# A hybrid encoder layer on one core: x also arrives transposed, one sum writes both attention patches, attention runs at another rate

## The chip, the cores and the metric

The kernel runs on one core of one Trainium2 chip. The metric is device microseconds from start to end of one execution. PE is the matrix engine, PEld its weight loads, DVE the vector engine, ACT the scalar engine, POOL GpSimd, and SP the engine that issues most DMAs.

## What is computed

One layer over T = 2048 tokens of D = 1024 channels, all in fp32:

```
h = rms_norm(x, norm_g)                    # mean of squares over the channels of a token
z = h @ w_in                               # 1024 x 10240
a, qkv, c, d, gates, merge = split(z)
y = [fourier(a), neighborhood_attention(q, k, v, rpb), conv_module(c), spatial_gating(d)]
merged = sum_n sigmoid(merge[n]) * ((y[n] * silu(gates[n])) @ w_branch[n])
out = rms_norm(x + merged @ w_out, final_g)
```

The attention works on a grid of 32 rows by 64 columns, 8 heads of 64 channels, with a window of 8 x 16 around each token.

## The kernel before

**Products.** Every large product is made of three matmuls on a high and a low part of each operand (`mm3`, line L238). `split` makes the parts: ACT casts the high one (L226), DVE subtracts it from the source for the low one (L227).

**The z phase** computes z in two halves of 1024 tokens, each in 20 blocks of 512 columns. A block takes seven products instead of eight, in the order B11, B21, T1, T2, B22, T3, T4; each has two parts of 12 matmuls of 512 columns (the first blocks, which come out turned, use 24 of 256). The names stand for quarters of normalised, transposed x and their differences T1 to T4: `hH` and `hL` are the two parts of such an operand, four tiles each. The operands are used by all blocks of a half. Weights arrive as `wq` tiles, get summed (L230) and split, five parts ahead.

**x in the kernel before.** `x_load` brings eight tiles `xn` of 128 tokens x 1024 channels. `x_square` (L468) squares a tile on ACT and sums along its row into `ss`; `x_rstd` makes 1 / root of it; `x_gain` spreads `norm_g` over the partitions with two matmuls against ones (L464); `x_scale` (L473) multiplies by both on DVE. An operand is then turned: for each of its four tiles, four transposes on PE (`x_turn_tile`, L504) fill one of three PSUM banks `p`, and `split` reads the bank. `first` places the steps in block 0 of the first half, before the products that need them (T2 is turned twice there). For the second half, block 17 of the first half loads and normalises x (`x_norm`, one step per turn of the side `xl`, whose rate is 2.0 per product step), GpSimd makes the differences, and `swap` and `swapped` turn the operands in the last block of the first half (19) and the first block of the second, as each old operand comes free.

**Order.** The code is written in program order; `tick` advances side work (a list of generators with rates) between matmuls, and a scheduler then fixes each engine's queue. Every engine works through its queue in order, SP's DMAs too.

**The y phase** projects eight blocks: for each half the branches 3, 2, 0, 1. A block is 8 x 4 steps of six matmuls (weights `yw`, gate tiles `sg`). Attention is side work here: each step advances it by `ATT_RATE[0]` pieces until block (0, 1), by `ATT_RATE[1]` after. A piece is the scores of one patch (L998), the turn of its probabilities (L1020), or the turn and `apply` (L1036). `apply` adds two partial results in `ot` and writes two patches of 8 x 16 tokens into the tile `ya` with two DVE sums (L1046, the patches stand reversed). The output of a head of the first half is stored to `yd` (`yd_77` is that of heads 6 and 7) and read back as `yL` by the next block; `fetch` advances attention until the heads that it wants are done. `gated` loads the gates of branch 1 into `bg`, which has one buffer.

## Time and profile before

| | |
|---|---|
| median of 3 runs | 2475.91 us (2474.22 to 2477.24) |
| the profiled execution, its own time | 2475.09 us |
| its span in the trace | 2473.3 us |
| mean granted clock of PE | 0.993 |
| PE busy | 2384.8 us, 96% of the span |
| DVE, ACT, POOL busy | 69%, 49%, 14% |

The span is what the trace covers; the rest of the execution's own time lies around it. The clock is a share of the full 2.4 GHz. A wait is named by the engine or DMA whose signal came last, and idle time of an engine other than the bottleneck costs nothing by itself. The mean of a matmul or a transpose is the time from its start to its modelled end; these overlap, so what one costs is read from the distance of starts.

### The profile page before, as it was taken

The numbers are of one execution on the slowest core, as the hardware profiler recorded it, in microseconds if no ns is written. First come the engines' busy times: TensorE is split into PE (matmuls) and PEld (weight loads), VectorE is DVE, ScalarE is ACT, GpSimd is POOL, SyncE is SP. The second block draws the span as 40 slices with busy tenths as digits, with TensorE's granted clock in tenths as the row PEclk, the third lists the DMA queues.
The fourth block names the chain that finished last, engine by engine and source line by source line (L and its number), as shares of the span: only waits on it lengthen the run. The fifth ranks groups of instructions, "written<-read, shape, count | busy, mean of one in ns | idle before, by whom it ended". The sixth has DMA issues, their size and how long they took to land. (4 is left out here: it accounts for less than half of the span.)

```text
span 2473.3 us, 34008 instructions
## 1 busy us (share of the span) xinstructions
PE 2384.8 (96%) x11804; PEld 1987.8 (80%) x11804; DVE 1699.2 (69%) x2945; ACT 1205.7 (49%) x2251; POOL 341.7 (14%) x290
## 2 busy tenths in 40 slices
PE   7999999999999999999999989999999999999998
PEld 6998778888877899878778867887777778778786
DVE  7585799997566637459979567673677775556542
ACT  5343545544584534354554465443666645654112
POOL 1000000000322100000000230001245433222220
PEclk9999999999999999999999999999999999999999
DMA  4353766655474335376774477777988978986776
GB/s 164 124 160 128 249 223 234 216 179 184 156 282 152 134 127 140 117 228 190 231 227 164 152 227 266 245 244 245 279 292 242 274 245 280 284 283 214 246 249 217
DMA packets 253015, 525.07 MB, mean 212 GB/s; under 512 B 26150, under 2 KB 120742, under 8 KB 252204
## 3 DMA queue, kind: packets, MB, share of 16 engines
q1 hardware_dynamic: 198572, 451.58, 56.2%
q10 hardware_dynamic: 54272, 71.32, 8.1%
q8 instruction: 93, 1.52, 0.3%
q14 instruction: 78, 0.64, 0.1%
HBM read 351.49 MB, written 171.31 MB: 211 GB/s over the span
## 5 line engine op out<-in xcount | busy, mean ns | idle before, releaser
L226 ACT CAST whi<-wq 128x512 fp32r<-128x512 f32 x560 | 347.0, 621 | 492.8 <-PE z L238 279.2
L227 DVE TENSOR_TENSOR wlo<-wq,whi 128x512 fp32r<-128x512 f32 x560 | 392.6, 703 | 268.3 <-ACT whi L226 258.8
L238 PE MATMUL z<-hH,whi 128*128 128x512 f32 x1088 | 427.7, 393 | 4.2 <-ACT b L374 4.0
L238 PE MATMUL z<-hH,wlo 128*128 128x512 f32 x1088 | 424.9, 391 | 3.2 <-DVE wlo L227 3.2
L238 PE MATMUL z<-hL,whi 128*128 128x512 f32 x1088 | 424.4, 390 | 0.0
L238 PE MATMUL b<-hH,whi 128*128 128x512 f32 x816 | 323.4, 396 | 16.1 <-DVE zu L233 15.9
L238 PE MATMUL b<-hH,wlo 128*128 128x512 f32 x816 | 319.7, 392 | 3.7 <-DVE wlo L227 3.7
L238 PE MATMUL b<-hL,whi 128*128 128x512 f32 x816 | 319.4, 391 | 0.0
L238 PE MATMUL z<-yH,yw 128*128 128x512 f32 x1024 | 305.8, 401 | 11.5 <-ACT yH L226 6.8
L786 DVE SCALAR_TENSOR_TENSOR acc<-hb,cw,acc 128x1009 f32<-128x1009 f32 (+1 forms) x240 | 306.9, 1282 | 2.0 <-ACT acc L782 1.5
L238 PEld LDWEIGHTS z<-hH,whi 128*128 128x128 f32 x1088 | 204.5, 188 | 47.5 <-ACT b L374 6.2
L238 PEld LDWEIGHTS z<-hH,wlo 128*128 128x128 f32 x1088 | 204.3, 188 | 46.8 <-DVE wlo L227 3.9
L238 PEld LDWEIGHTS z<-hL,whi 128*128 128x128 f32 x1088 | 204.5, 188 | 40.1
L238 PEld LDWEIGHTS z<-yH,yw 128*128 128x128 f32 x1024 | 191.8, 191 | 55.9 <-ACT yH L226 10.4
L238 PEld LDWEIGHTS b<-hH,whi 128*128 128x128 f32 x816 | 153.8, 188 | 54.7 <-DVE zu L233 16.1
L985 POOL TENSOR_TENSOR e<-mask,gt 128x512 f32<-128x512 bf16 x96 | 137.1, 1458 | 431.8 <-DMA gt<-in_rp_dram 360.3
L238 PEld LDWEIGHTS b<-hH,wlo 128*128 128x128 f32 x816 | 153.9, 189 | 36.8 <-DVE wlo L227 4.4
L238 PEld LDWEIGHTS b<-hL,whi 128*128 128x128 f32 x816 | 154.0, 189 | 30.4
L238 PE MATMUL z<-yL,yw 128*128 128x512 f32 x512 | 166.3, 401 | 2.7 <-DVE yL L227 2.4
L1007 ACT ACTIVATE sc<-sc,mn 128x512 f32<-128x512 f32 x128 | 92.5, 723 | 140.3 <-DVE mn L1004 140.2
L1004 DVE CUSTOM_DVE_ANT_0 sc<-p,e 128x512 f32<-128x512 f32 x128 | 87.1, 684 | 58.0 <-PE p L998 38.7
L238 PE MATMUL z<-yw,mH 128*128 128x512 f32 x384 | 119.7, 393 | 2.4 <-DMA yw<-wo 2.4
(228 smaller groups left out, 4123.2 us busy)
## 6 DMA issues: line engine op xcount, KB each, us to landing
wq<-in_wz_dram SPq DMA_DIRECT2D x140, 512.0 KB, 3.9
wk<-wq SPq DMA_DIRECT2D x80, 512.0 KB, 2.7
wq<-wk SPq DMA_DIRECT2D x80, 512.0 KB, 3.9
yw<-wb SPq DMA_DIRECT2D x64, 512.0 KB, 5.5
sg<-md SPq DMA_DIRECT2D x64, 512.0 KB, 5.0
yw<-wo SPq DMA_DIRECT2D x64, 512.0 KB, 4.2
vt<-vd SPq DMA_DIRECT2D x64, 320.0 KB, 7.4
md<-zs ACTq DMA_DIRECT2D x64, 256.0 KB, 3.5
```

Of the source, the lines that this page charges most:

```text
L226: nc.scalar.copy(hi, src)
L227: (eng or nc.vector).tensor_tensor(out=lo, in0=src, in1=hi.bitcast(F32), op=ALU.subtract)
L238: mm = lambda *a, **kw: self.nc.tensor.matmul(*a, skip_group_check=chained, **kw)
L786: nc.vector.scalar_tensor_tensor(out=a, in0=hb[:, j:j + n], scalar=self.cw[:, i, j:j + 1], in1=a, op0=ALU.mult, op1=ALU.add)
L985: nc.gpsimd.tensor_tensor(out=ev, in0=mv, in1=gv, op=ALU.subtract)
L1004: nc.vector.tensor_tensor_reduce(out=s2, in0=ps, in1=e, scale=1.0, scalar=3.0e38, op0=ALU.add, op1=ALU.min, accum_out=mn)
L1007: nc.scalar.activation(out=s2, in_=s2, func=AF.Exp, scale=-1.0, bias=mn[:, 0:1], accum_out=sm)
```

## The change

x comes a second time, transposed, as input `xt` (8 tiles of 128 channels x 2048 tokens), and `norm_g` as a constant of 128 x 8. The kernel's own input still gives the rows, but for the squares alone.

- `x_rows` loads `xt` into the eight `xn` tiles, in two parts of 512 tokens each.
- `x_square` loads a row tile of 128 x 512 into the ring `zs` (four buffers, shared with the results of the products) and squares it there; 16 of them fill `ss`.
- `x_rstd(c, banks)` adds the two sums of a token, takes root and reciprocal, multiplies the identity by the four columns (`d`, one more `zs` tile), and lets PE multiply ones by `d`, so that each partition has the factor of every token; ACT copies it to `t1`. At the start the product is made twice.
- `x_scale` multiplies an `xt` tile by the channel's gain (a scalar per partition) and by that factor.
- `x_split` splits from SBUF; the transposes and their PSUM banks are gone. The differences of operands are taken from the same places by the same engines.
- In the attention, `ph` and `pl` hold the two patches in reversed order, so that one sum of 64 x 16 x 16 writes both.
- `ATT_RATE[0]` goes from 1.6 to 1.75.

The diff, cut to its core:

```diff
...
 FFT_RATE = (1.15, 2.3)
-ATT_RATE = (1.6, 0.74)
+ATT_RATE = (1.75, 0.74)
 X_AT = 17
...
         x=np.asarray(x)[0],
+        xt=np.asarray(x)[0].T.reshape(KT, P, T),
         wz=wz, wb=wb, wo=wo, rp=rp,
-        ng=np.asarray(norm_g).reshape(1, D),
+        ng=np.asarray(norm_g).reshape(KT, P).T,
         cw=np.asarray(conv_w)[0].reshape(TAPS, 4, P).transpose(2, 1, 0),
...
+    def x_load(self, half):
+        self.t1 = self.xp.tile([P, 4, 512], F32, name="t1", tag="t1")
+        self.ss = self.zp.tile([P, 16], F32, name="ss", tag="ss", bufs=2)
+        self.xs = [self.xp.tile([P, 2, 512], F32, name="xn", tag="xn", bufs=8) for _ in range(KT)]
+        self.xt_at = half * HALF
+    def x_rows(self, k, c):
+        t0 = self.xt_at + 512 * c
+        self.load(self.xs[k][:, c], self.io["xt"][k, :, t0:t0 + 512])
+    def x_square(self, j, i):
+        t0 = self.xt_at + j * P
+        r = self.zs()
+        self.load(r, self.io["x"][t0:t0 + P, 512 * i:512 * i + 512])
+        self.nc.scalar.activation(out=self.t1[:, 0], in_=r, func=AF.Square, accum_out=self.ss[:, 8 * i + j:8 * i + j + 1])
+    def x_rstd(self, c, banks):
+        nc = self.nc
+        s, more = self.ss[:, 4 * c:4 * c + 4], self.ss[:, 8 + 4 * c:12 + 4 * c]
+        self.tt(s, s, more, ALU.add)
+        self.rstd(s, s, 1.0 / D)
+        d = self.zs()
+        for j in range(4):
+            at = slice(j * P, (j + 1) * P)
+            nc.vector.tensor_scalar(out=d[:, at], in0=self.ident, scalar1=s[:, j:j + 1], scalar2=None, op0=ALU.mult)
+        for bank in banks:
             ps = bank()
-            self.nc.tensor.matmul(ps, self.ones[0:1, :], row, start=True, stop=True)
-            self.nc.scalar.copy(self.t1[:, 2 + i], ps)
-    def x_square(self, j):
-        self.nc.scalar.activation(out=self.t1[:, 0:2].rearrange("p a c -> p (a c)"), in_=self.xs[j], func=AF.Square,
-                                  accum_out=self.ss[:, j:j + 1])
-    def x_scale(self, j, i):
-        xv = self.xs[j][:, 512 * i:512 * i + 512]
-        self.nc.vector.scalar_tensor_tensor(out=xv, in0=xv, scalar=self.ss[:, j:j + 1], in1=self.t1[:, 2 + i],
+            nc.tensor.matmul(ps, self.ones, d, start=True, stop=True)
+        nc.scalar.copy(self.t1[:, 2 + c], ps)
+    def x_scale(self, k, c):
+        xv = self.xs[k][:, c]
+        self.nc.vector.scalar_tensor_tensor(out=xv, in0=xv, scalar=self.ng[:, k:k + 1], in1=self.t1[:, 2 + c],
                                             op0=ALU.mult, op1=ALU.mult)
...
     def x_norm(self):
-        for j in range(8):
-            self.x_square(j)
-            yield
-        self.x_rstd(range(8))
-        for j in range(8):
-            for i in range(2):
-                self.x_scale(j, i)
+        for c in range(2):
+            for j in range(4 * c, 4 * c + 4):
+                for i in range(2):
+                    self.x_square(j, i)
+                    yield
+            for k in range(KT):
+                self.x_rows(k, c)
+                if k % 2:
+                    yield
+        for c in range(2):
+            self.x_rstd(c, (self.psp,))
+            yield
+        for c in range(2):
+            for k in range(KT):
+                self.x_scale(k, c)
                 yield
-    def x_parts(self, j, which):
-        a, b = self.xs[j], self.xs[4 + j]
-        return dict(B11=a[:, :512], B21=a[:, 512:], B12=b[:, :512], B22=b[:, 512:], T2=a[:, :512], T3=b[:, :512],
-                    T4=a[:, 512:], T1=self.t1[:, j])[which]
+    def x_parts(self, k, which):
+        a, b = self.xs[k], self.xs[4 + k]
+        return dict(B11=a[:, 0], B21=b[:, 0], B12=a[:, 1], B22=b[:, 1], T2=a[:, 0], T3=a[:, 1],
+                    T4=b[:, 0], T1=self.t1[:, k])[which]
     def x_sums(self, which, eng):
...
         a, b = dict(T1=("B12", "B11"), T3=("B22", "B12"), T2=("B22", "T1"), T4=("B21", "T2"))[which]
...
+    def x_split(self, which):
         self.X[which] = []
         for k in range(4):
-            if done:
-                ps = done[k]
-            else:
-                ps = self.psp()
-                for j in range(4):
-                    self.x_turn_tile(ps, which, j, k)
             hh = self.hp.tile([P, 512], F32R, name="hH", tag="hH" + which, bufs=4)
             hl = self.hp.tile([P, 512], F32R, name="hL", tag="hL" + which, bufs=4)
-            self.split(hh, hl, ps)
+            self.split(hh, hl, self.x_parts(k, which))
             self.X[which].append((hh, hl))
...
         self.ident = self.const("t_ident", [P, P])
-        self.x_load(0, range(1))
+        self.ng = self.const("ng", [P, KT])
+        self.x_load(0)
         self.rstd(self.ss[:, 0:1], self.eps, 1.0)
-        self.x_gain(self.psb)
-        self.x_load(0, range(1, 4))
         self.wq = {}
         self.w_gen, self.w_ahead = self.weights(), []
-        for i in range(4):
-            self.w_load(0, i)
-        self.x_load(0, range(4, 8))
         xl, mix, conv, fft, pre = (self.side(r) for r in (2.0, MIX_RATE, CONV_RATE[0], FFT_RATE[0], PRE_RATE))
...
         self.conv_side, self.fft_side = self.sides[2:4]
-        ps = [(self.psz if k < 2 else self.psp)() for k in range(4)]
         for j in range(4):
-            self.x_square(j)
-            self.x_rstd([j])
-            self.x_scale(j, 0)
-            for k in range(4):
-                self.x_turn_tile(ps[k], "B11", j, k)
+            for i in range(2):
+                self.x_square(j, i)
+        self.w_load(0, 0)
+        for k in range(4):
+            self.x_rows(k, 0)
+        for i in range(1, 4):
+            self.w_load(0, i)
+        for k in range(4, KT):
+            self.x_rows(k, 0)
+        self.x_rstd(0, (self.psb, self.psb))
         self.w_more()
-        xl.append(self.x_turn("B11", ps))
-        self.drain(xl)
-        for j in range(4):
-            self.x_scale(j, 1)
+        self.X["B11"] = []
+        split = self.x_split("B11")
+        for k in range(4):
+            self.x_scale(k, 0)
+            next(split)
+        for _ in split:
+            pass
         for _ in range(W_BUFS - 2):
             self.w_more()
+        for j in range(4, 8):
+            for i in range(2):
+                self.x_square(j, i)
+        for k in range(KT):
+            self.x_rows(k, 1)
         self.cw = self.const("cw", [P, 4, TAPS], self.zp)
...
             if i == 0:
-                xl.append(self.x_turn("B21"))
-                self.drain(xl)
-                for j in range(4, 8):
-                    self.x_square(j)
-                    self.x_rstd([j])
-                    self.x_scale(j, 0)
-                    self.x_scale(j, 1)
+                split = self.x_split("B21")
+                for k in range(4):
+                    self.x_scale(4 + k, 0)
+                    next(split)
+                for _ in split:
+                    pass
+                self.x_rstd(1, (self.psp,))
+                for k in range(KT):
+                    self.x_scale(k, 1)
                 xl.append(self.x_sums("T1", nc.vector))
                 self.drain(xl)
-                xl.append(self.x_turn("T1"))
+                xl.append(self.x_split("T1"))
             elif i == 1:
                 xl.append(self.x_sums("T2", nc.vector))
-                xl.append(self.x_turn("T2"))
+                xl.append(self.x_split("T2"))
             elif i < len(ORDER) - 1:
-                xl.append(self.x_turn(ORDER[i + 1]))
+                xl.append(self.x_split(ORDER[i + 1]))
                 if i == 2:
...
             if i:
-                xl.append(self.x_turn(ORDER[i - 1]))
+                xl.append(self.x_split(ORDER[i - 1]))
                 if i < 3:
...
                 self.drain(xl)
-                xl.append(self.x_turn(ORDER[-1]))
+                xl.append(self.x_split(ORDER[-1]))
         last = len(BLOCKS) - 1
...
                     open_pool("xp")
-                    self.x_load(1, range(8))
-                    self.x_gain(self.psp)
+                    self.x_load(1)
                     xl.append(self.x_norm())
...
             pt = pt.rearrange("p (b q) -> p b q", b=4)
-            nc.scalar.copy(ph[:, ri], pt)
-            nc.vector.tensor_tensor(out=pl[:, ri], in0=pt, in1=ph[:, ri].bitcast(F32), op=ALU.subtract)
+            nc.scalar.copy(ph[:, 1 - ri], pt)
+            nc.vector.tensor_tensor(out=pl[:, 1 - ri], in0=pt, in1=ph[:, 1 - ri].bitcast(F32), op=ALU.subtract)
             if ri == 1:
...
             for b in (1, 2, 3):
-                nc.tensor.matmul(po, vt[:, b], both[:, :, b:b + 4:3], start=b == 1, stop=False)
-            for ri, b, bi in ((0, 0, 0), (1, 4, 3)):
-                nc.tensor.matmul(po[:, :, ri], vt[:, b], pp[:, :, ri, bi], start=False, stop=ri == 1)
+                nc.tensor.matmul(po, vt[:, b], both[:, :, b - 1:b + 5:5], start=b == 1, stop=False)
+            for a, b, bi in ((1, 0, 0), (0, 4, 3)):
+                nc.tensor.matmul(po[:, :, a], vt[:, b], pp[:, :, a, bi], start=False, stop=a == 0)
             if cw == 0:
...
             nc.vector.tensor_tensor(out=t_, in0=po[0:64, 1], in1=t_, op=ALU.add)
-            for ri in range(2):
-                nc.vector.tensor_tensor(
-                    out=yt[:, 8 * ri:8 * ri + 8, 16 * cw:16 * cw + 16],
-                    in0=po[0:64, 0, ri, ::-1].rearrange("p (r c) -> p r c", r=8),
-                    in1=t_[:, ri, ::-1].rearrange("p (r c) -> p r c", r=8), op=ALU.add)
+            back = lambda t: t.rearrange("p a q -> p (a q)")[:, ::-1].rearrange("p (r c) -> p r c", r=16)
+            nc.vector.tensor_tensor(out=yt[:, :, 16 * cw:16 * cw + 16], in0=back(po[0:64, 0]), in1=back(t_), op=ALU.add)
             if cw == 3:
...
```

What moves in the queues shows at three places. **SP at the start**; `xn` are tiles of x (`xt` after), `zs` the ring, `wq` weights. Before:

```order
L210 DMA t_ident<-in_t_ident_dram 128x128
L210 DMA xn<-in_x_dram 128x1024
L210 DMA zs<-in_ng_dram 1x512 x2
L210 DMA xn<-in_x_dram 128x1024 x3
L210 DMA wq_262<-in_wz_dram 128x1024
```

After, from the row tiles of the second 512 tokens on (the first eight stand ahead, with four weight tiles and eight of `xt`):

```order
L211 DMA zs<-in_x_dram 128x512 [waits DMAHW6_49,Activation_49]
L211 DMA zs<-in_x_dram 128x512 [waits DMAHW7_49,Activation_49]
L211 DMA zs<-in_x_dram 128x512 [waits DMAHW0_49,Activation_49]
L211 DMA zs<-in_x_dram 128x512 [waits DMAHW1_49,DVE_49,PE_49]
L211 DMA xn<-in_xt_dram 128x512 [waits DMAHW2_49]
L217 DMA wk<-wq_286 128x1024 [waits DMAHW3_49,DVE_49]
L211 DMA zs<-in_x_dram 128x512 [waits DMAHW6_49,DMAHW4_49,Activation_49]
L211 DMA zs<-in_x_dram 128x512 [waits DMAHW7_49,DMAHW5_49,Activation_49]
```

The row tiles now wait for ACT's squares of the tiles before them in the ring; the fourth waits for DVE and PE, who fill and read the diagonal `d` in the same buffer, and the last four stand behind the store of a weight sum.

**ACT in block 17**, where the squares of the second half (L468, after L461) stand among the copies and casts of the products. Before:

```order
L468 ACTIVATE t_6990,ss<-xn 128x1024 [waits DMAHW4_49,DMAHW2_49,Pool_49]
L374 COPY b<-z 128x512 [waits PE_49]
L468 ACTIVATE t_6990,ss<-xn 128x1024 [waits DMAHW2_49,Activation_49]
L226 CAST whi<-wq_6676 128x512
L468 ACTIVATE t_6990,ss<-xn 128x1024 [waits DMAHW4_49,Activation_49]
```

After:

```order
L461 ACTIVATE t_6878,ss<-zs 128x512 [waits DMAHW3_49,DMAHW2_49,DMAHW5_49,DMAHW0_49,Pool_49]
L375 COPY b<-z 128x512 [waits PE_49]
L461 ACTIVATE t_6878,ss<-zs 128x512 [waits DMAHW3_49,Activation_49]
L461 ACTIVATE t_6878,ss<-zs 128x512 [waits DMAHW4_49,Activation_49]
L227 CAST whi<-wq_6738 128x512 [waits DVE_49,PE_49]
L461 ACTIVATE t_6878,ss<-zs 128x512 [waits DMAHW5_49,Activation_49]
```

There are 16 squares instead of 8, each behind its own load, with two between two casts where one stood. Later in the block, DVE's last scales (L480) have moved ahead of the two additions (L234) that free the banks of T3 and T4:

```order
L480 SCALAR_TENSOR_TENSOR xn<-xn,ng,t_6878 128x512 [waits DMAHW7_49]
L234 TENSOR_TENSOR zu<-z,zu 128x512 [waits PE_49]
L228 TENSOR_TENSOR wlo<-wq_7140,whi 128x512 [waits DMAHW4_49,Activation_49]
L480 SCALAR_TENSOR_TENSOR xn<-xn,ng,t_6878 128x512 [waits DMAHW0_49]
L480 SCALAR_TENSOR_TENSOR xn<-xn,ng,t_6878 128x512 [waits DMAHW1_49]
L234 TENSOR_TENSOR zu<-b,zu 128x512 [waits PE_49]
```

**SP at the entry into the last projection of the first half**; `yd_77` is the output of the last two heads, `vt`, `ks`, `qs` are operands of the next heads. Before:

```order
L216 DMA yd_77<-ya 64x1024
L210 DMA sg<-md_171 128x1024
L210 DMA yw<-wb_118 128x1024
L210 DMA yL<-yd_76 128x1024
L210 DMA yL<-yd_77 128x1024
L210 DMA vt<-vd 128x640
L210 DMA bg<-gd_92 128x1024
L210 DMA ks<-kd_65 64x1024
```

After:

```order
L211 DMA yw<-wb_118 128x1024
L211 DMA yL<-yd_76 128x1024
L217 DMA yd_74<-ya 64x1024
L211 DMA yL<-yd_77 128x1024
L211 DMA bg<-gd_92 128x1024
L211 DMA vt<-vd 128x640
L211 DMA sg<-md_173 128x1024
L211 DMA ks<-kd_65 64x1024
```

The store of the last heads stood four rows ahead of its load; it now stands 21 rows ahead, and in its place there is a store of the first head of the second half.

## Rows read from the trace of the kernel before

**Rows 1.** The page, its first and its sixth part (KB each, us to landing).

```profile
PE 2384.8 (96%) x11804; PEld 1987.8 (80%) x11804; DVE 1699.2 (69%) x2945; ACT 1205.7 (49%) x2251; POOL 341.7 (14%) x290
...
wq<-in_wz_dram SPq DMA_DIRECT2D x140, 512.0 KB, 3.9
```

**Rows 2.** Groups by line on PE: busy us, mean ns | idle before, releasers.

```profile
L504 PE MATMUL p<-t_ident,xn 128*128 128x128 f32 x200 | 33.7, 294 | 3.9 <-DVE hL L227 2.4 <-DVE xn L230 1.3 <-DVE xn L473 0.2
...
L504 PE MATMUL p<-t_ident,t 128*128 128x128 f32 x32 | 5.7, 299 | 2.1 <-DVE t L230 1.6 <-DVE hL L227 0.4
...
L504 PE MATMUL z<-t_ident,xn 128*128 128x128 f32 x8 | 2.7, 442 | 2.0 <-DVE xn L473 2.0
```

**Rows 3.** Timeline of PE, last block of the first half: start us, us.

```profile
792.11 0.39 PE L238 MATMUL z<-hL,whi 128*128 128x512 f32 x1
...
792.79 0.39 PE L238 MATMUL z<-hL,whi 128*128 128x512 f32 x1
...
839.85 0.60 PE L504 MATMUL p<-t_ident,xn 128*128 128x128 f32 x4
...
840.99 0.60 PE L504 MATMUL p<-t_ident,xn 128*128 128x128 f32 x4
```

**Rows 4.** Views of one line: ns min/median/max, first and last start.

```profile
L473 DVE SCALAR_TENSOR_TENSOR xn<-xn,ss,t x32: 734/744/1781, 9.9 to 758.6; 128x512 f32<-128x512 f32 x32
...
L227 DVE TENSOR_TENSOR wlo<-wq,whi x560: 621/684/1769, 13.8 to 1696.1; 128x512 fp32r<-128x512 f32 x187
...
L1046 DVE TENSOR_TENSOR ya<-p,ot x128: 259/273/284, 1748.9 to 2281.4; 64x128 f32<-64x128 f32 x128
```

**Rows 5.** Stretch 40 to 60: us, PE, PEld, DVE, ACT, POOL busy, clock, DMA, GB/s.

```profile
40.00:60.00 20.00, 16.37 (x116) 15.06 (x116) 18.54 (x23) 8.20 (x15) 6.59 (x4) 0.89 0.14 54
```

**Rows 6.** Timeline of the start, all engines.

```profile
5.20 1.06 ACT L468 ACTIVATE t<-xn 128x1024 f32<-128x1024 f32 x1 [2.88 <-DMA xn<-in_x_dram]
...
5.43 3.75 PE L464 MATMUL b<-zs,ones 1*128 1x512 f32 x4 [5.43 <-DMA zs<-in_ng_dram]
...
16.31 0.58 PE L238 MATMUL z<-whi,hH 128*128 128x256 f32 x1
```

**Rows 7.** Timeline of the first block, all engines.

```profile
37.24 0.38 PE L238 MATMUL z<-whi,hH 128*128 128x256 f32 x1 [0.46 <-ACT hH L226]
...
41.55 4.67 DVE L230 TENSOR_TENSOR xn<-xn,t 128x512 f32<-128x512 f32 x4
...
42.48 6.59 POOL L230 TENSOR_TENSOR xn<-xn 128x512 f32<-128x512 f32 x4 [42.04 <-DVE xn L230]
...
84.26 0.59 ACT L719 COPY zs<-b 128x512 f32<-128x512 f32 x1
```

**Rows 8.** Timeline of block 17, PE and DVE.

```profile
725.96 0.39 PE L238 MATMUL z<-hH,whi 128*128 128x512 f32 x1
...
737.18 1.98 PE L464 MATMUL p<-zs,ones 1*128 1x512 f32 x4 [1.08 <-DMA zs<-in_ng_dram]
...
755.69 0.50 PE L238 MATMUL z<-hH,wlo 128*128 128x512 f32 x1 [2.72 <-DVE wlo L227]
...
759.98 0.51 PE L238 MATMUL b<-hH,wlo 128*128 128x512 f32 x1 [0.82 <-DVE wlo L227]
...
763.36 0.68 DVE L233 TENSOR_TENSOR zu<-b,zu 128x512 f32<-128x512 f32 x1
```

**Rows 9.** Stretches at the entry into the last projection, columns as in rows 5.

```profile
1965.00:1980.00 15.00, 13.42 (x58) 9.75 (x58) 11.79 (x30) 9.55 (x20) 10.29 (x7) 0.89 0.97 296
...
1990.00:2000.00 10.00, 8.91 (x27) 6.91 (x28) 6.48 (x9) 2.28 (x3) 3.33 (x2) 0.66 0.76 270
sum 45.00, PE 35.45 PEld 25.70 DVE 35.69 ACT 26.70 POOL 15.31; mean PE 8.86 PEld 6.42 DVE 8.92 ACT 6.68 POOL 3.83
```

**Rows 10.** Timeline there, the queue of SP and PE.

```profile
1984.42 0.33 SPq L210 DMA_DIRECT2D bg<-gd  x1
...
1991.09 0.77 PE L998 MATMUL p<-ks,qs 128*128 128x512 f32 x1 [3.75 <-DMA qs<-qd]
```

More of the change, by code (lines that the diff above doesn't have):

```diff
@@ L442, in rstd @@
         self.nc.vector.reciprocal(out, out)
-    def x_load(self, half, js):
-        if js[0] == 0:
-            self.xs = []
-            self.t1 = self.xp.tile([P, 4, 512], F32, name="t1", tag="t1")
-            self.ss = self.zp.tile([P, 8], F32, name="ss", tag="ss", bufs=2)
-        for j in js:
-            t0 = half * HALF + j * P
-            xt = self.xp.tile([P, D], F32, name="xn", tag="xn", bufs=8)
-            self.load(xt, self.io["x"][t0:t0 + P, :])
-            self.xs.append(xt)
@@ L456, in x_gain @@
-    def x_gain(self, bank):
-        row = self.zs()[0:1]
-        for i in range(2):
-            if i:
-                row = self.zs()[0:1]
-            self.load(row, self.io["ng"][:, 512 * i:512 * i + 512])
-            ps = bank()
-            self.nc.tensor.matmul(ps, self.ones[0:1, :], row, start=True, stop=True)
-            self.nc.scalar.copy(self.t1[:, 2 + i], ps)
-    def x_square(self, j):
-        self.nc.scalar.activation(out=self.t1[:, 0:2].rearrange("p a c -> p (a c)"), in_=self.xs[j], func=AF.Square,
-                                  accum_out=self.ss[:, j:j + 1])
@@ L483, in x_norm @@
             yield
-        self.x_rstd(range(8))
-        for j in range(8):
-            for i in range(2):
-                self.x_scale(j, i)
+        for c in range(2):
+            for k in range(KT):
+                self.x_scale(k, c)
                 yield
-    def x_parts(self, j, which):
-        a, b = self.xs[j], self.xs[4 + j]
-        return dict(B11=a[:, :512], B21=a[:, 512:], B12=b[:, :512], B22=b[:, 512:], T2=a[:, :512], T3=b[:, :512],
-                    T4=a[:, 512:], T1=self.t1[:, j])[which]
+    def x_parts(self, k, which):
+        a, b = self.xs[k], self.xs[4 + k]
+        return dict(B11=a[:, 0], B21=b[:, 0], B12=a[:, 1], B22=b[:, 1], T2=a[:, 0], T3=a[:, 1],
+                    T4=b[:, 0], T1=self.t1[:, k])[which]
@@ L498, in x_sums @@
         a, b = dict(T1=("B12", "B11"), T3=("B22", "B12"), T2=("B22", "T1"), T4=("B21", "T2"))[which]
[L499 to L500 removed]
+        for k in range(4):
+            self.tt(X(k, which), X(k, a), X(k, b), ALU.subtract, eng)
             yield
[L503 to L506 removed]
+    def x_split(self, which):
         self.X[which] = []
         for k in range(4):
[L509 to L514 removed]
             hh = self.hp.tile([P, 512], F32R, name="hH", tag="hH" + which, bufs=4)
             hl = self.hp.tile([P, 512], F32R, name="hL", tag="hL" + which, bufs=4)
[L517 removed]
+            self.split(hh, hl, self.x_parts(k, which))
             self.X[which].append((hh, hl))
@@ L577, in first @@
             if i == 0:
-                xl.append(self.x_turn("B21"))
-                self.drain(xl)
-                for j in range(4, 8):
-                    self.x_square(j)
-                    self.x_rstd([j])
-                    self.x_scale(j, 0)
-                    self.x_scale(j, 1)
+                split = self.x_split("B21")
+                for k in range(4):
+                    self.x_scale(4 + k, 0)
[5 more added lines that the diff above has]
+                    self.x_scale(k, 1)
                 xl.append(self.x_sums("T1", nc.vector))
                 self.drain(xl)
-                xl.append(self.x_turn("T1"))
+                xl.append(self.x_split("T1"))
             elif i == 1:
                 xl.append(self.x_sums("T2", nc.vector))
-                xl.append(self.x_turn("T2"))
+                xl.append(self.x_split("T2"))
             elif i < len(ORDER) - 1:
-                xl.append(self.x_turn(ORDER[i + 1]))
+                xl.append(self.x_split(ORDER[i + 1]))
                 if i == 2:
```

8 lines of the change are left out of this document (removed).

## The prediction

> **What bounds the kernel now.** The page's first line comes first: PE is busy for 2384.8 us of 2473.3, 96% [rows 1]. So only what takes time from PE's own queue, or removes one of its waits, moves the end. The groups by line on PE come second: the transposes of x are 200 + 32 + 8 = 240 instructions [rows 2]. Their mean of 294 ns is a latency and not a price, because they overlap. The price is read from the timeline of PE. In a plain stretch three matmuls of 512 columns lie 0.68 us apart [rows 3]. With four transposes between them the period is 840.99 - 839.85 = 1.14 us, so four cost 0.46 us, 0.114 each. Third come the stretches in which PE is not full: the start, block 17 of the first half (where the second half of x is normalised), and the entry into the last projection of the first half.
>
> **The change, part by part.** The profiled execution took 2475.09 us, span 2473.3 and 1.8 around it, and lies 0.8 under the median of the runs, 2475.91. The sum is made against 2475.09.
>
> *The second half's turns.* The last block of the first half and the first of the second hold 112 of the 240 transposes. PE is full there (period above), and ACT's casts and DVE's subtractions stay, only with a source in SBUF. DVE's splits that read two SBUF inputs already take 0.68 us [rows 4]. So 112 x 0.114 = **-12.8 us**. Bounds: -12.8, and -8 if half a dozen splits come late.
>
> *The first block* holds the other 128 transposes (T2 is turned twice), 16 before the first product. Removing 112 inside it would give another 12.8, but PE isn't the bound there: DVE is busy 18.54 of 20 us [rows 5]. So I follow the chain.
> First product: before, it starts at 16.31 [rows 6]. After, x rows arrive in quarter tiles through a ring of four buffers. The first tile of 512 KB is squared from 5.20, and takes 1.06 us [rows 6]; for 256 KB I take 4.3 and 0.7 us. Four squares end at 7.1; the next four rows leave only as buffers come free, two weight casts stand among their squares, and the last ends at about 11.7. Then root and reciprocal 0.5, four diagonals 0.8 (about 0.2 each, estimated under the 0.27 of a 64x128 sum [rows 4]), two ones-matmuls 3.75 (four passes at the low clock [rows 6]), a copy 0.6, a scale 0.74 [rows 4], a cast 0.6: 18.7, so +2.4.
> T1: SP's order shows the rows of tokens 512 to 1023 behind a buffer that holds the diagonal (free at 16.8) and behind a store that waits for DVE's first weight sum (about 23). The last four rows leave after that and are squared by 33, between B21's casts; 0.5 + 0.8 + 1.0 + 0.6 make the second factor ready at 36, eight scales take 5.5, one sum and cast 1.3: T1 starts at 42.9, where it started at 37.24 [rows 7], +5.7.
> Then it turns. T2's transposes are gone with the PSUM buffers they waited for; by DVE's order T2 ends at 59.4. B22, T3 and T4 are 144 matmuls at 0.12, 17.3 us, and 3 more because DVE makes T2's parts a second time: the block ends at 79.7, before at 84.26 [rows 7]. **-4.5**. Bounds: -19 (all 112 transposes, 12.8, and some 6 us of PE's waits: 20 - 16.37 = 3.6 in the stretch of [rows 5], the rest ahead of it), and +6 (T1's delay is never caught up).
>
> *Block 17.* Before, PE lost 1.08 + 2.72 + 0.82 in waits and 1.98 for two matmuls [rows 8]. After, it runs two ones-matmuls of the same length in other places. ACT's 16 squares (0.7 each, 11 us; before 8 of 1.25) each wait for a row of x, and ACT's order puts the copies and casts of PE's products between them. Following that order from 725.96, where the second product starts [rows 8], with 12 matmuls of 0.227, 2.72 us, a product, the second root comes at 753.5, the second diagonal at 755.6, the second factor at 758.2. Six of the last eight scales, slowed to 1.1 us by GpSimd's sums, stand in DVE's queue ahead of the addition that frees T3's bank. T4 waits for it until 768.6; before, that addition ran at 763.36 [rows 8]. PE has run 1.8 us of the next block ahead. **+3**. Bounds: -6.6 (every wait and both matmuls hidden), and +8.
>
> *Attention at 1.75.* The rate itself moves work, and adds none. Between 1955 and 2000 PE is busy 35.45 of 45 us, 9.55 idle; the granted clock averages 0.89 in 15 us and 0.66 in 10, so another 1.7 + 3.4 us are lost at 1.2 GHz [rows 9]. Here head 7 is finished 1.75 steps before block (0, 1) wants it, the queue of SP stands behind the one buffer of bg until 1984.42, and PE waits 3.75 for the next queries [rows 10]. At 1.75 head 7 is 9.5 steps ahead, and the scores that waited are spread in PE's order. I take off 8 of the 14.6 and add 2 for a denser first half, in which DVE and ACT are 7 to 9 tenths busy. **-6**. Bounds: -14.6, and +5 (half as many waits again over 1737 to 1955).
>
> *One sum for both patches* removes 64 of 128 additions of 0.27 us and makes the others about 0.41: DVE saves 64 x 0.14 = 9 us, all beside PE. 0, bounds 0 and -2.
>
> Sum: -12.8 - 4.5 + 3 - 6 = -20.3, so 2475.1 - 20.3 = **2454.8 us**, say 2455.
>
> **Rivals.**
> *The x rows hold ACT up (slower).* Place: ACT's queue in block 17 and in the first block. A 512 KB load lands after 3.9 us [rows 1]. If a square costs ACT its whole wait, 3.9 + 0.7, sixteen cost 74 us; the block covers 38 and the casts made ahead four products, 10.9, so PE stands 25 us. In the first block eight squares take 37 where I gave 20: +17. With -12.8 and -6 the sum is +23, 2498. It decides from 49 / 16 = 3.1 us a square; four buffers in flight make it about 1.2. 6%.
> *The start and block 17 eat half of it.* Both at their upper bounds: -12.8 + 6 + 8 - 6 = -4.8, 2470, about no change. For it: DVE is nearly full in the first block, and SP waits there in order. 6%.
> *Attention gives nothing.* DVE is the bound in the first half at either rate: -12.8 - 4.5 + 3 + 2 = -12.3, 2463. For it: most waits there name DVE or ACT. 18%.
> *GpSimd blocks the splits.* Before, four sums on DVE beside GpSimd's T4 sums took 4.67 us, 1.17 each instead of 0.67 [rows 7]; the splits of x read one operand from PSUM then and two from SBUF now. If each of the first block's four T2 splits waits 1.08 (the longest split of the source view is 1.77 [rows 4]), T2 ends 4.3 later: 2459. In the last block eight such waits fit into DVE's idle time. 10%.
> The Trainium skill, page "SBUF — State Buffer" (section "Who interferes with whom"), says that VectorE instructions with two SBUF inputs and GpSimd instructions that read SBUF lock each other out, and it speaks against this change; by it the sum would be that rival's 2459, by splits at the length that they have now 2455. The trace agrees for sums (1.17 us [rows 7]), and no run here shows it for these splits yet.
> *More comes back.* First block and attention near their lower bounds, -12.8 - 12 + 3 - 12 = -34, 2441. 8%.
>
> **How the numbers follow.** The forecast has 52%, the rivals 6, 6, 18, 10 and 8. The range reaches from 2442 to 2468: it takes in the two small rivals and leaves out the slower one, most of the no-change one and half of the best. About 0.2%, 5 us, is what a measurement of this kernel can tell from no change; under 2471 is faster. Faster 0.88, within 0.2% 0.06, slower 0.06.
>
> **What would show it.** The 112 right: in the last block of the first half PE's matmuls stand 0.227 us apart without a gap. The first block right: T1's first matmul at 41 to 45, the block's last copy at 77 to 82; if the copy stands after 85, the chain through the ring was under-priced. Block 17 right: two ones-matmuls without a long wait before them, and one wait of PE of 5 to 9 us on DVE near T4. Attention right: no wait on qs at the entry of the last projection, and PE idle under 6 us in the 45 around it. Wrong altogether: ACT's idle time before its squares over 30 us and PE waiting for casts behind them.

## The result, and the profile after

The changed kernel is slower: 2500.44 us median of 4 runs (2497.85 to 2508.36), against 2475.06 of the kernel before, a ratio of 1.0108 (95% interval 1.0083 to 1.0132). The forecast was 2455. The page after begins:

```profile
PE 2368.9 (95%) x11566; PEld 1968.8 (79%) x11566; DVE 1698.2 (68%) x2896; ACT 1221.8 (49%) x2286; POOL 337.7 (14%) x290
```

Beside [rows 1], PE has 238 instructions fewer and 15.9 us less to do, and yet the span has grown from 2473.3 to 2499.0 us. So PE waits longer. Where, is read by laying the same points of the program side by side: the first copy of a block on ACT (blocks 1, 17, 19 of the first half, 1 of the second), and the first and a late matmul of the projections on PE. Timelines before, then after:

```profile
87.03 0.58 ACT L374 COPY b<-z 128x512 f32<-128x512 f32 x1
...
726.16 0.57 ACT L374 COPY b<-z 128x512 f32<-128x512 f32 x1
...
811.42 0.58 ACT L374 COPY b<-z 128x512 f32<-128x512 f32 x1
...
901.12 0.57 ACT L374 COPY b<-z 128x512 f32<-128x512 f32 x1 [1.14 <-PE z L238]
...
1710.69 0.50 PE L238 MATMUL z<-yH,yw 128*128 128x512 f32 x1 [1.62 <-ACT yH L226]
...
2443.65 0.39 PE L238 MATMUL z<-yw,mL 128*128 128x512 f32 x1
```

```profile
91.06 0.58 ACT L375 COPY b<-z 128x512 f32<-128x512 f32 x1
...
728.14 0.57 ACT L375 COPY b<-z 128x512 f32<-128x512 f32 x1 [0.71 <-PE z L239]
...
827.35 0.58 ACT L375 COPY b<-z 128x512 f32<-128x512 f32 x1
...
907.05 0.57 ACT L375 COPY b<-z 128x512 f32<-128x512 f32 x1 [1.19 <-PE z L239]
...
1714.17 0.50 PE L239 MATMUL z<-yH,yw 128*128 128x512 f32 x1 [1.62 <-ACT yH L227]
...
2469.13 0.39 PE L239 MATMUL z<-yw,mL 128*128 128x512 f32 x1
```

| Stretch | before, us | after, us | difference | forecast |
|---|---|---|---|---|
| start to block 1 | 87.03 | 91.06 | +4.0 | -4.5 |
| to block 17 | 639.13 | 637.08 | -2.1 | 0 |
| block 17 and 18 | 85.26 | 99.21 | +14.0 | +3 |
| turns of the second half | 89.70 | 79.70 | -10.0 | -12.8 |
| to the projections | 809.57 | 807.12 | -2.5 | 0 |
| projections and attention (y phase) | 732.96 | 754.96 | +22.0 | -6 |
| rest | 29.65 | 29.87 | +0.2 | 0 |

Such a table carries a noise of its own: stretches whose code and order are the same differ by up to 7 us between the runs below, so only what several runs show is built upon. And 1.7 of the 4.0 us in its first row are no loss of PE: the copy that marks block 1 stands on ACT behind a cast that waits for a load, 2.89 us where it was 1.15 before, and the next row gives it back. The last copy of the first block [rows 7] comes 2.3 us later, and PE's matmuls are 2.4 us late from there on.

**The first block.** PE's waits, then the operand splits on DVE and the sums on POOL (after):

```profile
21.51 0.39 PE L239 MATMUL z<-whi,hH 128*128 128x256 f32 x1 [2.11 <-ACT hH L227]
...
45.53 0.58 PE L239 MATMUL z<-whi,hH 128*128 128x256 f32 x1 [5.69 <-ACT hH L227]
...
57.92 0.58 PE L239 MATMUL b<-whi,hH 128*128 128x256 f32 x1 [2.61 <-ACT hH L227]
61.77 0.58 PE L239 MATMUL b<-whi,hL 128*128 128x256 f32 x1 [2.63 <-DVE hL L228]
```

```profile
55.41 8.12 DVE L228 TENSOR_TENSOR hL<-xn,hH 128x512 fp32r<-128x512 f32 x8
```

```profile
50.40 9.56 POOL L231 TENSOR_TENSOR xn<-xn 128x512 f32<-128x512 f32 x4 [49.96 <-DVE xn L231]
```

The eight splits by length (ns min/median/max), and the block's last copy on ACT:

```profile
L228 DVE TENSOR_TENSOR hL<-xn,hH x8: 677/679/1758, 55.4 to 62.8; 128x512 fp32r<-128x512 f32 x8
...
86.54 0.59 ACT L730 COPY zs<-b 128x512 f32<-128x512 f32 x1
```

The first product starts at 21.5 instead of 16.3 [rows 6], T1 at 45.5 instead of 37.2 [rows 7]. Then the eight splits of T2 (its four, made twice) take 8.12 us beside GpSimd's sums. The mean of 1.02 us hides two lengths: three of them take 1.75 us each, in turn with a sum of 1.71 on GpSimd, and five the usual 0.68 [rows 4]. GpSimd's four sums grow from 6.59 [rows 7] to 9.56 us; 4.53 of that is the first one, beside a run of DVE's own sums. The Trainium skill, page "SBUF — State Buffer" (section "Who interferes with whom"), says that VectorE instructions with two SBUF inputs and GpSimd instructions that read SBUF shut each other out; the trace agrees, with 8.12 us for what would be 5.4. PE waits 2.6 us twice for these parts, and from 57.0 to 67.2, with the waits and behind them, its granted clock is 0.50, 1.2 GHz (stretch after, columns as in rows 5):

```profile
57.00:67.20 10.20, 6.65 (x29) 6.36 (x30) 10.20 (x15) 4.37 (x8) 2.96 (x2) 0.50 0.11 43
```

**Block 17.** ACT, PE and DVE after:

```profile
734.42 0.63 ACT L461 ACTIVATE t<-zs 128x512 f32<-128x512 f32 x1 [3.17 <-DMA zs<-in_x_dram]
...
735.05 0.58 ACT L375 COPY b<-z 128x512 f32<-128x512 f32 x1
```

```profile
735.68 0.50 PE L239 MATMUL z<-hH,whi 128*128 128x512 f32 x1 [2.14 <-ACT b L375]
758.39 1.12 PE L475 MATMUL p<-zs,ones 128*128 128x512 f32 x2 [3.57 <-DVE zs L472]
...
777.88 0.80 PE L239 MATMUL z<-hH,wlo 128*128 128x512 f32 x1 [5.33 <-DVE wlo L228]
```

```profile
757.46 0.88 DVE L472 TENSOR_SCALAR zs<-t_ident,ss 128x128 f32<-128x128 f32 x4 [6.88 <-DMA xn<-in_xt_dram]
...
769.05 7.09 DVE L480 SCALAR_TENSOR_TENSOR xn<-xn,ng,t 128x512 f32<-128x512 f32 x6
776.07 0.68 DVE L234 TENSOR_TENSOR zu<-z,zu 128x512 f32<-128x512 f32 x1
776.67 1.15 DVE L228 TENSOR_TENSOR wlo<-wq,whi 128x512 fp32r<-128x512 f32 x1
```

A square waits 3.17 us for its row tile, and the copy behind it on ACT releases PE only after it. Later six scales, three of 0.74 and three of 1.75 us, stand in DVE's queue ahead of the addition and the weight part that PE wants: 5.33 us. Over the whole stretch, blocks 17 and 18, PE's time without work grows from 4.6 to 15.3 us, and its granted clock falls from 1.00 to 0.93 (before, then after):

```profile
726.16:811.42 85.26, 80.64 (x355) 65.19 (x354) 50.44 (x64) 43.32 (x76) 14.20 (x8) 1.00 0.56 209
...
728.14:827.35 99.21, 83.95 (x343) 66.23 (x342) 53.97 (x74) 49.53 (x98) 13.84 (x8) 0.93 0.63 222
```

**The y phase.** Stretches before, then after, cut at the same matmuls: the second and third projection of the first half, and the first two weight tiles of the last one (columns as in rows 5).

```profile
1780.95:1867.39 86.44, 83.66 (x415) 67.02 (x413) 64.26 (x160) 55.96 (x116) 36.61 (x25) 0.98 0.94 281
1867.39:1956.97 89.58, 84.97 (x430) 67.75 (x430) 68.25 (x181) 62.49 (x129) 38.05 (x27) 1.00 0.82 245
1956.97:1996.83 39.86, 30.70 (x126) 21.87 (x125) 30.55 (x69) 24.25 (x48) 13.36 (x9) 0.87 0.81 256
```

```profile
1788.12:1885.76 97.64, 91.05 (x448) 72.36 (x447) 70.33 (x177) 67.90 (x142) 32.73 (x24) 0.97 0.84 261
1885.76:1982.91 97.15, 89.12 (x431) 70.48 (x431) 68.45 (x168) 62.30 (x129) 42.47 (x32) 0.96 0.78 231
1982.91:2027.57 44.66, 33.31 (x139) 23.38 (x138) 31.81 (x74) 27.89 (x56) 11.02 (x9) 0.89 0.80 249
```

In the second projection PE's idle time rises from 2.8 to 6.6 us; the rest of its growth is mostly attention moved here from later (448 instructions instead of 415). The third has the same work and takes 7.6 us more: idle time 4.6 to 8.0, clock 1.00 to 0.96. At the entry into the last projection nothing has been gained: 44.7 us for 39.9 with 13 more instructions, idle time 11.4 for 9.2. PE's waits there after the change (compare [rows 10]):

```profile
2000.69 0.63 PE L1031 MATMUL p<-t_ident,sc 128*128 128x128 f32 x4 [1.42 <-DVE mn L1015]
...
2022.78 0.98 PE L239 MATMUL z<-yH,yw 128*128 128x512 f32 x2 [3.61 <-ACT yH L227]
```

The wait of 3.75 us for the next queries is gone, as forecast. Waits for reductions and for the last gated operand stand in its place. Over the whole y phase PE's time without work grows from 29.7 to 42.6 us, and its mean clock falls from 0.99 to 0.98. Two results of DVE account for that growth: the row reduction of the scores (`mn`) and the low part of the turned probabilities (`pp`). PE's waits for them in the y phase (us in total, times, longest), before and then after:

```profile
PE p L1020 <- DVE mn L1004: 3.6, 6, 0.9
PE p L998 <- DVE pp L1023: 2.0, 3, 1.2
```

```profile
PE p L1031 <- DVE mn L1015: 8.8, 9, 1.8
PE p L1048 <- DVE pp L1035: 5.8, 4, 2.4
```

With the smaller rows these two grow from 7.9 to 22.4 us, although DVE is busy for only 452 of the 755 us.

### The profile page after: what moved, and what is told of

The parts are those of the page before. It is cut to its first block, busy times and chain, and to the rows that moved or that the text cites. A ratio compares the mean times of both kernels' runs of the same rounds, so it can differ in the third digit from the quotient of the medians.

```text
span 2499.0 us, 33600 instructions
## 1 busy us (share of the span) xinstructions
PE 2368.9 (95%) x11566; PEld 1968.8 (79%) x11566; DVE 1698.2 (68%) x2896; ACT 1221.8 (49%) x2286; POOL 337.7 (14%) x290
## 4 chain that ended last, share of the span: by engine, by line
PE 58%; DVE 19%; DMA 10%; issue 6%; ACT 5%; POOL 2%; SPq 1%; ACTq 0%; DVEq 0%; POOLq 0%
PE z L239 35%; PE b L239 15%; DVE acc L797 6%; DVE wlo L228 3%; PE p L239 3%; PE p L1009 1%; PE p L1031 1%; DMA pw<-in_wb_dram 1%; DMA wq<-in_wz_dram 1%; PE p L1048 1%; DVE zu L234 1%; DVE hL L228 1%; DVE xn L480 1%; DMA zs<-in_x_dram 1%; POOL e L996 1%
## 5 line engine op out<-in xcount | busy, mean ns | idle before, releaser
L996 POOL TENSOR_TENSOR e<-mask,gt 128x512 f32<-128x512 bf16 x96 | 130.1, 1388 | 409.0 <-DMA gt<-in_rp_dram 349.3
```

Source lines behind the costliest of these rows:

```text
L996: nc.gpsimd.tensor_tensor(out=ev, in0=mv, in1=gv, op=ALU.subtract)
```

## The experiments

**The three parts alone.** Theory "rate": the constant 1.75 brings the loss of the y phase. Rivals: the one sum, or the shift by the z phase.

```diff
-ATT_RATE = (1.6, 0.74)
+ATT_RATE = (1.75, 0.74)
```

> The kernel before with the attention rate of the first half at 1.75 instead of 1.6, nothing else. In the trace after, the projections of the first half (first to last matmul of the y phase) account for 22.5 of the 25 us lost, and the z phase for 3.5. Theory 'rate': this constant alone brings that loss, 2475 + 22 = 2497, with PE's waits on DVE and ACT in the attention growing from 21 to about 30 us and stretches at 1.2 GHz behind them. Rival 'sum': the one sum of both patches brings it, then this kernel stays at 2465 to 2477. Rival 'shift': neither does it alone, the attention is late because the z phase ends in another state; then 2470 to 2480 here and in the run with the sum alone.

Measured: 1.0088 (1.0071 to 1.0106); y phase 752.8 us for 733.0. The rate alone does it, and PE's waits for `mn` and `pp` are 21.7 us here, nearly the 22.4 of the whole change.

The sum alone (the edits of `turn` and `apply`):

> The kernel before with the two patches in reversed order and one sum of 64 x 16 x 16 for both, nothing else. Theory 'rate': 2473 to 2477, no change, as 64 sums of 0.41 us in place of 128 of 0.27 lie beside PE's work. Rival 'sum': 2490 to 2500, because the longer sum holds up the subtraction that the next matmuls wait for.

Measured: 1.0022 (1.0006 to 1.0037), y phase 743.1. A small loss where none was expected, nowhere near the rival's. (The traced execution is one of the slower ones, 2488.0 at a median of 2482.5.)

The transposed x alone:

> The changed kernel with the attention of the kernel before (two sums, rate 1.6): the transposed x alone. Theory 'rate': 2475 + 3.5 = 2478 to 2480, the gain of 10 us in the last block of the first half and the first of the second being eaten by 4 in the first block and 14 in block 17. The prediction's own terms for this part gave 2475 - 14.3 = 2461. Rival 'shift': 2490 or more, with the loss in the attention although its code is the old one.

Measured: 1.0044 (1.0028 to 1.0059), between theory and rival: block 17 and 18 lose 15.6 us, the turns give back 10.0, the y phase takes 735.7. The attention is not late by itself.

The change with the rate undone:

> The changed kernel with the rate of the first half back at 1.6: transposed x and one sum. Theory 'rate': 2477 to 2480, as the x part alone. Rival 'sum': about 2500, as with the whole change.

Measured: 1.0059 (1.0041 to 1.0076), y phase 739.9 for 755.0. More than theory said, mostly since the transposed x alone already costs 0.44%, 11 us, and not the expected 3 to 5; the sum adds 0.15%. Still, nearly half of the whole loss is gone with one constant. The parts don't add up exactly: 1.0044, 1.0022 and 1.0088 would give 1.0154, the whole is 1.0108.

**The x part.** The diagonals out of the ring:

```diff
-        self.nc.scalar.activation(out=self.t1[:, 0], in_=r, func=AF.Square, ...
+        self.nc.scalar.activation(out=r, in_=r, func=AF.Square, ...
...
-        d = self.zs()
+        d = self.t1[:, c]
```

> The changed kernel, but the diagonals lie in two free quarters of t1 and the squares overwrite their own row tile, so that the ring zs carries rows alone. In the trace after, the first root of block 17 is done at 747 and its diagonal starts at 757.5, when the thirteenth square has freed the buffer; the scales then come in one lump beside GpSimd's sums, and the block loses 14.4 us against before. Theory 'ring': with the diagonal free of the ring, block 17 loses 6 or less, the fourth row tile of the second 512 tokens no longer waits for PE in the first block, and the total falls from 2500 to about 2490. Rival 'rows': ACT's waits for the row tiles themselves (9.6 us in seven waits) set the block; then it still loses 12 or more and the total stays within 3 us of 2500.

Measured: 1.0095 (1.0073 to 1.0116); block 17 and 18 still lose 11.9 us. The diagonal is made at 749.5 now, but ACT's copy of the factor stands behind a square that waits for its row (timeline of ACT):

```profile
757.44 0.63 ACT L461 ACTIVATE zs<-zs 128x512 f32<-128x512 f32 x1 [2.89 <-DMA zs<-in_x_dram]
...
758.58 0.58 ACT L476 COPY t<-p 128x512 f32<-128x512 f32 x1
```

The diagonal's place in the ring was not the cause; the rival, which named the rows, misses its bounds by only 0.1 us in the block and 0.3 in the total. The rows out of the ring as well:

```diff
-        r = self.zs()
+        r = self.xs[2 * (j % 4) + i][:, 1]
```

> The changed kernel with the diagonals in t1 as in the run before, and the row tiles of x loaded into the halves of the eight xn tiles that are still free, so that eight of them can be under way and none uses the ring zs. In the run with the diagonal alone moved, block 17 still lost 13 us: ACT waited 9.3 us for row tiles, and PE 3.4 us for a copy that stood behind such a square. Theory 'rows': ACT's waits for row tiles in block 17 fall under 4 us, PE's wait for that copy goes, and the block loses 4 to 8 us; the total is 2490 to 2495. Rival 'lump': PE's wait of 4.7 us behind six scales beside GpSimd's sums, and the low clock after it, carry most of it; the block still loses 10 or more, 2497 to 2503.

Measured: 1.0066 (1.0051 to 1.0081); block 17 and 18 lose 4.1 us instead of 14.0 (89.4 us, where the six runs with that part unchanged have 98.1 to 102.0), total 2497.9 us beside a before of 2480.9 on that chip. Theory "rows" holds in size, though ACT still waits 6.0 us for rows in four waits, and PE 1.75 us for the copy. The lump on DVE is one wait of PE of 4.14 us (PE, same run):

```profile
739.23 0.50 PE L239 MATMUL z<-hH,whi 128*128 128x512 f32 x1 [1.75 <-ACT b L375]
...
773.14 0.80 PE L239 MATMUL z<-hH,wlo 128*128 128x512 f32 x1 [4.14 <-DVE wlo L228]
```

T2 split once:

```diff
-                xl.append(self.x_split(ORDER[i + 1]))
+                if i > 2:
+                    xl.append(self.x_split(ORDER[i + 1]))
```

> The changed kernel without the second splitting of T2 in the first block (the same operand was split twice, before as after). After, eight splits of T2 take 8.12 us on DVE beside GpSimd's sums, 1.02 each, and PE waits 2.6 + 2.6 us there. Theory 'shared port time': four of them gone save 3 to 4 us, and the first block ends that much earlier: 2496 to 2497. Rival: PE waits for the first four alone, and the copies were off the path: 2500.

Measured: block 1 begins at 88.16 instead of 91.06, 2.9 us earlier (the five runs with that block unchanged have 90.8 to 92.0), in size about what the theory said; the total, 1.0084 (1.0059 to 1.0109), is too wide to show it. But the time beside GpSimd did not go: of the four splits that are left three still take 1.75 us each (ns min/median/max).

```profile
L228 DVE TENSOR_TENSOR hL<-xn,hH x4: 681/1756/1762, 55.7 to 60.7; 128x512 fp32r<-128x512 f32 x4
```

What went are four plain splits, 2.4 us of DVE's queue, since they stand 0.60 us apart.

**The rate: depth of the chain, masks, density.** `ATT_TURN = 3` becomes 4:

> The changed kernel with the probabilities turned four pieces of work behind their scores instead of three (the rate stays 1.75). The y phase takes 755 us after and 733 before, from first to last matmul. Theory 'latency': at 1.75 the three pieces last 9% less time than the chain of reduction, exponential, reciprocal and copy needs; with four the y phase comes back to 740 or less, the total to about 2485. Rival 'bursts': scores stand still while the masks come late from GpSimd, then come in a lump that DVE can't serve; the y phase stays at 750 or more.

Measured: 1.0147 (1.0125 to 1.0169), y phase 765.6. More distance made it worse, which speaks against the latency of three pieces.

All sums of the merged branches on DVE:

```diff
-                    self.tt(mg[dt][c], mg[dt][c], sc, ALU.add, nc.gpsimd if c else None)
+                    self.tt(mg[dt][c], mg[dt][c], sc, ALU.add)
```

> The changed kernel with all sums of the merged branches on DVE, none on GpSimd, so that GpSimd makes only the masks there. After, DVE is idle for 27 us for masks that stand behind such a sum in GpSimd's queue (before: 19). Theory 'bursts': these waits fall under 10 us and the y phase from 755 to about 742. Rival 'DVE is full': eight more sums of 0.68 us a block, 5 us, make DVE the bound and the y phase longer, 760 to 770.

Measured: 1.0084 (1.0059 to 1.0110), y phase 752.2. DVE's waits for masks fell from 27.1 to 7.5 us, and 2.7 us of 22 came back, less than such stretches differ by themselves. Neither side of the expectation is met: masks are a small part, and DVE took more work without harm.

A lower rate, on the mended kernel below:

> The half-mended kernel (2470, ratio to before 0.9955) with the attention of the first half at 1.5 instead of 1.6. In the orders of PE the projections of blocks 1 and 2 then hold at most five turns of attention between two weight tiles; at 1.6 three hold 7 or 8, at 1.75 more hold 6 to 8, and in the traces the tiles with six or more carry nearly all of the lost time. Against that, the heads of the first half are not done when the last projection wants them, so that attention is pulled forward there (nine turns in its second tile). Theory 'density': blocks 1 and 2 lose 5 to 8 us less than at 1.6, the entry 3 to 6 us more, and attention left for the second half costs up to 6; y phase 728 to 737 against 734 now, total 2464 to 2473. Rival 'entry': what counts is that the heads are ready before the last projection; then the entry loses 10 us or more and the y phase is 743 or longer, total 2479 or more.

Measured: 0.9974 (0.9960 to 0.9988), y phase 743.0 for 734.1. The trace is of the slowest of 12 executions, 2482.2 us; their median is 2474.9, between theory and rival, 5 us above the rate of 1.6. Theory "density" gets no support: the traces had shown that weight tiles with many turns of attention lose most (time less their matmuls at full clock, first three projections of five runs: 0.7 us on the mean with up to three turns, 2.4 with six or seven, 6.4 with eight), but thinning them gave nothing in the second and third projection, the entry lost about what it did, and the second half lost more. PE's waits for `mn` and `pp` are 19.5 us here too, at the lower rate.

**Added work.** The last question was whether an engine is full where attention is dense. Control: the mended kernel at 1.75.

> The half-mended kernel with the attention rate at 1.75: control for the next runs. From the rate alone on the kernel before: y phase 752 to 756 against 734 at 1.6, total 2488 to 2493.

Measured: 1.0053 (1.0033 to 1.0073), y phase 759.6 for 734.1. PE and DVE work through the y phase in the same order as in the run with the rate alone, and PE's waits for `mn` and `pp` grow from 7.6 to 21.6 us: one order, measured in two kernels.

```diff
-            for ri in range(2):
+            for ri in (0, 1, 0, 1):
```

> The half-mended kernel (rate 1.6, y phase 734, total 2470), with each of the two sums that write the patches made twice: 128 more DVE instructions of 0.27 us, 35 us, 18 of it in the projections of the first half. Theory 'DVE': where attention is dense DVE has no time left, so half or more of it comes out at the end, y phase 750 or more, total 2486 or more. Theory 'ACT' or 'chain' (this sum stands at the end of the chain, and nothing but the next head's store waits for it): 734 to 740, total 2470 to 2476.

Measured: 0.9999 (0.9988 to 1.0010), y phase 747.6: a third of the 35 us comes out, more than "ACT" and "chain" said and less than "DVE".

> The same doubled sums at rate 1.75. Theory 'DVE': the denser attention has still less DVE time left, so the added work costs more than at 1.6: y phase 772 or more. Theory 'ACT' or 'chain': 754 to 760.

Measured: 1.0005 (0.9994 to 1.0016), y phase 753.8. "DVE" (772 or more) falls: with 35 us more for DVE the kernel at 1.75 is faster than its control, by 0.5%, and beside the same sums at 1.6 (0.9999) the rate costs nothing that shows. Stretches about the third projection and the entry (from the middle of the third projection's first weight tile, the same matmuls in both), control and then with the sums doubled:

```profile
1880.44:1982.18 101.74, 91.48 (x452) 71.85 (x450) 76.07 (x195) 69.02 (x142) 36.68 (x29) 0.99 0.78 237
1982.18:2011.58 29.40, 22.86 (x97) 16.84 (x98) 21.84 (x55) 18.38 (x37) 9.70 (x8) 0.88 0.78 242
```

```profile
1884.03:1981.29 97.26, 87.78 (x428) 68.46 (x426) 75.41 (x209) 61.92 (x128) 36.07 (x26) 0.98 0.81 236
1981.29:2009.66 28.37, 21.95 (x105) 15.87 (x104) 23.22 (x62) 19.48 (x40) 9.70 (x8) 1.00 0.70 212
```

PE holds 428 instructions instead of 452 in the first stretch, since the scheduler has placed the attention otherwise, and the clock in the second is 1.00 instead of 0.88.

> The half-mended kernel (rate 1.6) with the copy of the turned probabilities made twice on ACT for the first of two patches: 64 more instructions of 0.59 us, 38 us. Theory 'ACT': y phase 755 or more. Theory 'DVE': the subtraction behind each copy comes 0.6 us later but DVE's own time is unchanged: 734 to 742. Theory 'chain': as the copy stands in the middle of the chain, between the turn and the product, 740 to 752, more than for the doubled sums.

Measured: 0.9964 (0.9949 to 0.9979), y phase 739.8. With 38 us more ACT the total is that of the kernel without (0.9955) within the intervals. "ACT" falls, "DVE" is met, and "chain" misses by 0.2 us.

So none of the three theories holds in all three runs. What is shown: the constant 1.75 changes no work, only the order in the engines' queues, and two such orders, of the whole change and of the rate alone, cost 15 to 26 us of the y phase; a third, with the doubled sums, costs 6 us there and nothing in the total. In the two dear orders PE waits 11 to 14 us longer for `mn` and `pp`. Why DVE answers later there, though it is not full, is not settled. That it is a matter of single places in the order and of no resource is likely, but not shown.

**Versions with what was learnt.** Rows and diagonals apart, scales among the squares, T2 once, old attention:

> Transposed x for both halves with rows and diagonals apart from the ring, the scales of the first 512 tokens placed among the squares of the second, T2 split once, and the attention of the kernel before (two sums, rate 1.6). By the stages measured so far: first block +1, block 17 +4 to +8, the turns of the second half -10, attention 0; theory 'stages' gives 2475 - 5 to 2475, 2470 to 2475. Rival: the transposed x costs DVE and ACT more wherever it stands, and the total stays at 2482 or more, as little better than the transposed x alone.

Measured: 0.9977 (0.9967 to 0.9987), 2474.7 us. Block 17 and 18 lose 1.5 us, the turns give 10.0, the first block costs 1.8: together -6.7, and 0.23% of 2480.9 is -5.7. The stages add up within their noise.

> The first half as in the kernel before (rows, transposes on PE), except that T2 is split and turned once; the second half from transposed x as in the mended kernel; the attention of the kernel before. By stages: first block -2 to -3, block 17 +4 to +8, turns -10, so 2475 - 4 to -9: 2466 to 2471. Rival as for the mended kernel: 2476 or more, if block 17 alone eats the turns.

Measured: 0.9955 (0.9941 to 0.9970), 2469.95 us beside a before of 2480.89: the lowest ratio of all, ahead of both kernels. The first block is 2.2 us shorter than before (T2 once), block 17 and 18 lose 0.8.

## Why the prediction was wrong

The largest miss is the attention, 28 us between forecast and measurement, then block 17 with 11 and the first block with 7 to 9.

- **The turns of the second half** (-12.8): right in kind, -10.0 in the change and in every run with transposed x. The term was a little too large: the 96 transposes of the first half's last block took 47.67 - 38.1 = 9.5 us (168 matmuls of 0.227 make 38.1), 0.099 each and not 0.114, and one new wait of 1.13 us behind DVE stands there.
- **The first block** (-4.5): wrong, +2.3 by its last copy (86.54 where 79.7 was worked out). T1 came 2.6 us later than worked out: the first eight squares ended at 13.8 and not at 11.7, the last at 35.1 and not at 33, so the chain through the ring was under-priced, as the forecast's own sign (a copy after 85) says. Then T2, worked out to end 16.5 us after T1's start, took 24.0; 3 of these 7.5 us more had been put behind T2, for its second making. The step that failed is the price of T2's eight splits, and with it the clock: three of them were held by GpSimd's sums, 3.2 us, and behind PE's waits for them matmuls ran at 1.2 GHz, a term that the chain did not have. The rival "GpSimd blocks the splits" had the mechanism and 4.3 us, and was given 10%. It should have been the forecast, since [rows 7] showed 1.17 us for the same engines at the same place.
- **Block 17** (+3, bounds to +8): wrong, +14. The lump of scales ahead of T3's addition was foreseen, and PE's wait there (5.33 us) lies in the 5 to 9 that were named as a sign. What failed is the chain before it: each square was taken to cost its own time, and the loads behind the shared ring to be timely. The second factor came at 769.0 instead of 758.2, PE had a wait of 3.57 us before the ones-matmuls where none was expected, and the fall of the clock to 0.93 was not in the sum. The slower rival named the place and the cause, ACT's queue behind row tiles, but as 25 us here and 17 in the first block; that its total, 2498, meets the result is luck: the attention lost what those two did not.
- **Attention** (-6, bounds to +5): wrong, +22 with the sum. The single wait that was read from the trace went away as foreseen, but the entry took 44.7 us for 39.9, with PE idle for 11.4 us where the sign was under 6 in 45. The step that failed is the sentence that the waiting scores would be spread: a rate was priced by the one wait it removes, and the new order of everything else was bounded by half of the waits seen. In its place the runs show a new order in which PE waits 14.5 us more for `mn` and `pp`; why these come late there stays open. The "attention gives nothing" rival reached only +2.
- **One sum** (0): +5 us by its ratio (1 to 9). DVE's saving was real (1027 to 963 instructions in the y phase) and worth nothing.

## What to carry to other kernels

Price a constant that steers a scheduler by a run and not by the wait that it is meant to remove: a changed order has a price of its own, here 15 to 26 us of the y phase and not the 6 us gain. A load that feeds an in-order engine must not share a small ring with results, since each wait then stands in front of whatever else that engine owes the bottleneck. And where two engines already slow each other in the trace, that row is the forecast for the next pair put beside them.

## What was unexpected of the hardware

Waits of one to four microseconds cost more than their length where PE's granted clock falls behind them. Waits of PE late in the attention, in the changed kernel, and the clock (last column but two) ahead of them and behind:

```profile
2203.32 0.63 PE L1031 MATMUL p<-t_ident,sc 128*128 128x128 f32 x4 [0.99 <-DVE mn L1015]
2206.38 0.96 PE L1048 MATMUL p<-pp,vt 128*128 128x512 f32 x3 [2.43 <-DVE pp L1035]
2209.38 1.12 PE L1031 MATMUL p<-t_ident,sc 128*128 128x128 f32 x4 [0.90 <-DVE mn L1015]
```

```profile
2195.00:2205.00 10.00, 7.72 (x36) 5.99 (x36) 5.11 (x17) 9.88 (x18) 0.00 (x0) 1.00 0.33 121
2205.00:2220.00 15.00, 11.80 (x36) 8.62 (x37) 8.40 (x17) 10.60 (x19) 3.94 (x4) 0.66 0.69 212
```

A mean of 0.66 over 15 us is ten of them at 1.2 GHz. Over the whole run the mean went from 0.993 to 0.984.
